# A decoder block in split-float products: two more units with Strassen steps, a new opening order, and a reordered last normalisation

## The chip, the cores and the metric

The kernel runs on one core of one Trainium2 chip. The metric is the device time of one execution in microseconds; three runs of the kernel before gave 2355.65 to 2356.98 with a median of 2356.65. Engines are named as in the profile: PE is the tensor engine (PEld its weight loads), DVE the vector engine, ACT the scalar engine, POOL the GpSimd engine, SP the engine that issues most DMAs.

## The reference, cut to what matters

```python
h = rmsnorm(x, norm_w)                                   # x: 256 tokens x 4096
proj = einsum('bsd,de->bse', h, w_in)                    # 4096 -> 20480
u_p, z_p, u_c, b_c, c_c, z_c, g_logit = split(proj)      # six of 2048, one of 8192
y_pool = causal_multiscale_pool(u_p, pool_w, pool_scale) * silu(z_p)
v = c_c * u_c                                            # causal convolution of width 3
y_conv = b_c * (conv_b + sum(conv_w[k] * shifted(v, k))) * silu(z_c)
br = einsum('bsnc,ncd->bsnd', stack(y_pool, y_conv), w_branch)
merged = sum(sigmoid(g_logit + gate_b) * br, over the two branches)
x = x + einsum('bsd,de->bse', merged, w_out)
return rmsnorm(x, final_norm_w)
```

All arrays are float32. `rmsnorm(x, w)` is `x * rsqrt(mean(x*x) + 1e-6) * w` over the 4096 channels of a token.

## The kernel before

**Products.** Each float32 operand is split into a high and a low part of the PE's rounded float format, and a product is three matmuls: high x high, high x low, low x high. ACT writes the high parts (`highs`), DVE subtracts to get the low parts (`lows`). A matmul is 128x128 weights against 128x512.

**Units and steps.** The work is a list of units, each 1024 output columns for all 256 tokens: cz0, cb0, cu0, cc0, then cz1 to cc1 (convolution branch: z, b, u and c columns), pz0, pu0, pz1, pu1 (pooling branch), eight gate units g, eight branch units b0_0, b1_0, b0_1 and so on, and four output units o0 to o3. A unit of the input or output product has 16 steps, a branch unit has 8; a step takes 256 rows of the weight matrix. The unit's string of letters says which steps are plain pairs (`P`: 8 block products, 24 matmuls) and which are one Strassen-Winograd step (`S`: 7 block products, 21 matmuls). An S step costs DVE and ACT more: besides the highs and lows of the weight tile (three ring cells) it needs four sums of its quarters in the tile `parts`, and their highs and lows (four more cells). The activations' side of an S step needs its own sums (`x_sums` in the opening, `Fill` later).

**The bank scheme.** Plain products accumulate in four banks (`sums`), S steps in these and in four more (`shared`). When a unit's products for a bank are complete, ACT copies the bank out (`evacuate` for the first four, into E or Y; `copy_corners` for the others, into J), DVE adds up J (`corner_sums`), and `combine` adds J to the unit's result: on DVE, or for units marked `late` by two accumulating DMAs on POOL (`gather`). Units marked `late` apply the input norm's factor `rin` afterwards; the first unit, which has no S step, applies it in `evacuate`.

**Order.** Every engine runs its instructions in the order written; the program is one long list made at build time. After each group of three matmuls `after_group` writes what has become due: bank copies, corner sums, then one entry of the `queue` of the previous unit's closing work (an entry, a tick, per six matmuls), one step of a `Fill`, and then `pump`, which issues weight loads (three raw tiles of 1 MiB) and the preparation of coming steps, up to four ahead, as far as the ring's 15 cells reach: four for a P, three and then four for an S. A P step gives back a cell after its second, fourth, sixth and eighth group, an S step one after each group. In a unit's last step `pump` is left out for some groups so that bank copies are not queued behind preparation:

```python
after_group(u, g[0], st, st is u.steps[-1] and st.kind == "P" and 3 <= i < len(gs) - 1)
```

Units with an `urgent` function prepare only `lead` steps ahead during their last step.

**The opening.** The first unit also prepares the activations: `x_direct` for the eight pairs that stay plain (two ACT copies and two DVE instructions), `x_scale` on ACT and `x_sums` on DVE for the eight Strassen operands (number 8 to 15), each written one step ahead. `FIRST` is the order of the 16 operands. In steps 4, 7, 10 and 13 a quarter of x is fetched into E, in steps 6, 9, 12 and 15 squared and summed (one half on ACT, one on DVE), and behind step 15 `root` computes `rin`.

**The end.** The last unit's last three steps are done token half by token half (t = 0, 1), the second one also column half by column half. `finish_half` adds a bank to E, squares it on ACT with a sum into `ossq`, and multiplies by the final weights; `finish` turns the five partial sums into `rout` by reduce, scale, square root and one Newton step, scales four column quarters by it and writes them.

Of the kernel before, what the change touches and what calls it, by code (L numbers as in the profile page):

```python
# [15 lines left out]
P = 128  # L16
# [34 lines left out]
def hybrid_block(ctx: ExitStack, tc: tile.TileContext, x, xc, prm, rows_in, w_in, pool_w, w_branch, w_out, out):  # L51
# [488 lines left out]

    def silu_y(late):
        def silu(t):
            act(Y[:, t], Y[:, t], AF.Silu, **(dict(scale=rin[:, t:t + 1]) if late else {}))
        return gap(18 if late else 3) + [lambda: silu(0), None, lambda: silu(1)]

# [4 lines left out]
    def conv_units(c, first):  # L550
# [7 lines left out]
        def c_epi(u):  # L558
            def inner(j):
                if j == 3:  # L560
                    for i in range(4):
                        act(chan(E)[:, 2 * i:2 * i + 2], bankview(i))

            def outer(j):
                act(chan(J)[:, 2 * j:2 * j + 2], bankview(j))

            def taps(j):
                v, y = chan(E)[:, 2 * j:2 * j + 2], chan(Y)
                for i in range(2):
# [12 lines left out]
            return items + [None, lambda: mul(chan(E), chan(J), chan(Y)), lambda: put(y_d[1, c], chan(E))]  # L582

        u = in_unit(f"cz{c}", base + 3 * HALF, lambda u: silu_y(u.late) + (gap(4) + side_items(ND - 1) + side_items(ND - 2) if first else []),
                    FIRST if first else SIX5, dst=Y)
        u.late = not first
        in_unit(f"cb{c}", base + HALF, b_epi, TEN if c else NINE_A).late = True
        u = in_unit(f"cu{c}", base, lambda u: rescale(Y), NINE, dst=Y)
        u.late = True
        in_unit(f"cc{c}", base + 2 * HALF, c_epi, NINE_A).urgent = lambda: mul(E, E, Y)  # L590

    def pool_units(c):
        u = in_unit(f"pz{c}", HALF + c * NU, lambda u: silu_y(True) + gap(4) + band_items(c), HOST if c else SIX5, dst=Y)
        u.late = True
# [187 lines left out]
    class Fill:  # L782
        def __init__(self, o, src, free, ready):
            self.o, self.free, self.ready, self.src = o, free, ready, src
            self.at = self.st = None
            self.phase = self.due = 0
# [26 lines left out]
    def pop_fill(force=None):  # L813
        now[0] += 1
        for f in list(fills):
            if f.at is not None and f.free() and (now[0] >= f.at + LANDING or f.o is force):
                if f.advance(f.o is force):
                    break
# [53 lines left out]
    for _ in range(WARM):  # L872
        pin(nc.tensor.matmul(shared(3)[:, 0:2 * P], warm[:, 0:P], warm, start=True, stop=True))

    def rstd_of(q, r, name):
        a = q.shape[1]
        m = sb(f"{name}_m", [P, a])
        s = sb(f"{name}_s", [P, a])
        pin(nc.vector.tensor_reduce(out=m, in_=q, axis=mybir.AxisListType.X, op=ALU.add))
        pin(nc.vector.tensor_scalar(out=m, in0=m, scalar1=1.0 / D, scalar2=EPS, op0=ALU.mult, op1=ALU.add))  # L880
        act(s, m, AF.Sqrt)
        pin(nc.vector.reciprocal(out=r, in_=s))
        mul(m, m, r)
# [181 lines left out]
    def queue_fills():  # L1065
        for n in range(2):
            for i in [s.op for s in names[f"b{n}_0"].main]:
                j = y_ops[n].index(i)
                fills.append(Fill(i, y_d[n, j // 4][:, j % 4].rearrange("p k t -> p (k t)"), freed(i),
                                  lambda: True))  # L1070
# [27 lines left out]
    for u in units:  # L1098
# [28 lines left out]
        for st in u.steps:  # L1127
# [5 lines left out]
            if state["now"] == OPENED:  # L1133
                opening.close()
                sums = ctx.enter_context(tc.tile_pool(name="parts", bufs=1)).tile([P, 4, NH], F32, name="parts")
                open_side()
# [38 lines left out]
    def finish_half(t, n):  # L1175
        cs = slice(n * NH, (n + 1) * NH)
        add(E[:, t, cs], PE_[t][n], E[:, t, cs])
        act(sa[:, 4 * n:4 * n + 4].rearrange("p o c -> p (o c)"), E[:, t, cs], AF.Square,
            accum_out=ossq[:, t, 3 + n:4 + n])
        mul(rest[:, t, cs], E[:, t, cs], Y[:, 0, cs])  # L1180

    def finish(t):
        r = rout[:, t:t + 1]
        rstd_of(ossq[:, t:t + 1], r, f"rout{t}")
        for c in range(4):
            v = rest[:, t] if c == 3 else parked[c][:, t]
            if c == 1:
                act(v, v, scale=r)
            else:
                pin(nc.vector.tensor_scalar(out=v, in0=v, scalar1=r, scalar2=None, op0=ALU.mult))  # L1190
        for c in (1, 0, 2, 3):
            v = rest[:, t] if c == 3 else parked[c][:, t]
            queue_ = nc.scalar if c == 1 else nc.sync
            pin(queue_.dma_start(of[t * P:(t + 1) * P, c * NU:(c + 1) * NU], v))

# [51 lines left out]
```

## Time and profile before

| | |
|---|---|
| median of 3 runs | 2356.65 us |
| the profiled execution | 2356.82 us |
| its span, first to last instruction | 2354.7 us |
| mean granted PE clock | 0.999 |
| busy: PE, DVE, ACT, POOL | 2340.7, 2217.8, 1542.9, 139.0 us |
| matmuls | 10424 |
| DMA, mean over the span | 242 GB/s |

The profile is of one execution. A timeline row has the start, the time, the engine, the line, the operation with its tiles, the count of merged instructions, and in brackets the idle time of that engine in front of it with what ended it. A row of the chain of waits has start, time, engine and tile. A row of the windows view has the stretch, its length, then busy time and count for PE, PEld, DVE, ACT and POOL, the granted clock, and the DMA share and rate. Most helpers record under one line each: L58 is any ACT instruction, L61 any DVE tensor-tensor instruction, L73 scalar-tensor-tensor, L1026 the matmuls.

### The profile page before, as it was taken

The page shows a single profiled execution, that of the slowest core. Times are in us where ns is not written, and L with a number is a line of the kernel's source. Part 1 is how long each engine was busy: PE and PEld are TensorE (multiplying, and loading weights), DVE is VectorE, ACT ScalarE, POOL GpSimd, SP SyncE. Part 2 cuts the span into 40 slices and gives each one's busy share as a digit, 9 for nine tenths or more (in the row PEclk, how much of TensorE's full clock was granted, in tenths as well). Part 3 has the DMA queues.
Part 4 walks back from the last instruction along what each step waited for, and adds up shares of the span by engine and source line. Part 5 has one row for each costly group of instructions (what it writes and reads, how often), then busy time and mean ns, then how long its engine had stood idle before and what let it go on. Part 6 is the DMA issues. An engine that isn't in the chain of part 4 may idle for free.

```text
span 2354.7 us, 28337 instructions
## 1 busy us (share of the span) xinstructions
PE 2340.7 (99%) x10424; PEld 1938.7 (82%) x10424; DVE 2217.8 (94%) x2454; ACT 1542.9 (66%) x1841; POOL 139.0 (6%) x195
## 2 busy tenths in 40 slices
PE   9999999999999999999999999999999999999998
PEld 7888888888888888888888888888888888888886
DVE  8899989999979979979999999998999899999998
ACT  6666756766656666666677767677666566566664
POOL 0000000000001000100000000001101001000000
PEclk9999999999999999999999999999999999999999
DMA  9667655776656656656787787778767678767877
GB/s 351 231 234 248 217 201 215 251 232 233 222 207 216 219 196 213 220 198 222 242 258 254 256 265 246 250 267 283 258 225 247 254 247 282 250 206 263 260 255 279
DMA packets 95387, 569.44 MB, mean 242 GB/s; under 512 B 10320, under 2 KB 10576, under 8 KB 34832
## 3 DMA queue, kind: packets, MB, share of 16 engines
q1 hardware_dynamic: 69824, 485.39, 56.7%
q0 software_dynamic: 24848, 81.01, 13.7%
q8 instruction: 81, 1.33, 0.2%
q10 hardware_dynamic: 576, 1.24, 0.1%
q14 instruction: 58, 0.48, 0.1%
HBM read 521.46 MB, written 25.17 MB: 232 GB/s over the span
## 4 chain that ended last, share of the span: by engine, by line
PE 97%; DVE 1%; DMA 0%; ACT 0%; issue 0%; DVEq 0%; SPq 0%; ACTq 0%
PE sums L1026 70%; PE shared L1026 25%; PE shared L676 1%; PE shared L462 1%; DVE ring L61 1%; DMA raw<-in_w_branch_dram 0%; DVE parts L61 0%; DMA raw<-in_w_in_dram 0%; ACT ring L58 0%; DVE arena L61 0%; PE shared L652 0%; DVE J L61 0%; ACT E L58 0%; PE shared L653 0%; PE shared L655 0%
## 5 line engine op out<-in xcount | busy, mean ns | idle before, releaser
L1026 PE MATMUL sums<-ring,arena 128*128 128x512 f32 x7011 | 1640.7, 390 | 1.9 <-ACT E L58 1.1
L1026 PEld LDWEIGHTS sums<-ring,arena 128*128 128x128 f32 x7011 | 1315.3, 188 | 275.5 <-ACT E L58 1.5
L61 DVE TENSOR_TENSOR ring<-raw,ring 128x1024 fp32r<-128x1024 f32 (+2 forms) x887 | 962.2, 1104 | 70.4 <-ACT ring L58 69.5
L58 ACT ACTIVATE ring<-raw 128x1024 fp32r<-128x1024 f32 (+3 forms) x682 | 785.5, 1192 | 210.2 <-PE sums L1026 98.5
L58 ACT ACTIVATE ring<-parts 128x512 fp32r<-128x512 f32 (+1 forms) x683 | 510.4, 761 | 510.2 <-DVE parts L61 438.3
L1026 PE MATMUL shared<-ring,arena 128*128 128x512 f32 x2241 | 541.1, 389 | 0.0
L61 DVE TENSOR_TENSOR ring<-parts,ring 128x1024 fp32r<-128x1024 f32 (+1 forms) x475 | 524.5, 1146 | 8.7 <-ACT ring L58 8.7
L1026 PEld LDWEIGHTS shared<-ring,arena 128*128 128x128 f32 x2241 | 420.6, 188 | 87.3
L61 DVE TENSOR_TENSOR parts<-parts,raw 128x512 f32<-128x512 f32 x444 | 303.3, 683 | 0.0
L61 DVE TENSOR_TENSOR parts<-raw 128x1024 f32<-128x1024 f32 x222 | 270.2, 1217 | 10.9 <-DMA raw<-in_w_in_dram 6.0
L61 DVE TENSOR_TENSOR J<-J 128x512 f32<-128x512 f32 (+1 forms) x90 | 78.1, 868 | 6.0 <-ACT J L58 2.8
L1026 PE MATMUL sums<-ring,last_pair 128*128 128x512 f32 x306 | 76.2, 389 | 0.0
L58 ACT ACTIVATE J<-shared 128x512 f32<-128x512 f32 x128 | 69.5, 601 | 1.6
L1026 PEld LDWEIGHTS sums<-ring,last_pair 128*128 128x128 f32 x306 | 57.4, 188 | 11.9
L85 POOL DMA_DIRECT2D E<-J x28 | 34.2, 1463 | 479.5 <-ACT ring L58 300.1
L1026 PE MATMUL shared<-ring,last_pair 128*128 128x512 f32 x216 | 51.9, 389 | 0.0
L1026 PE MATMUL shared<-ring,side 128*128 128x512 f32 x207 | 50.7, 389 | 0.0
L1026 PEld LDWEIGHTS shared<-ring,last_pair 128*128 128x128 f32 x216 | 40.5, 188 | 8.4
L1026 PEld LDWEIGHTS shared<-ring,side 128*128 128x128 f32 x207 | 38.9, 188 | 8.1
L58 ACT ACTIVATE E<-sums 128x512 f32<-128x512 f32 x76 | 41.8, 592 | 4.5 <-PE sums L1026 2.7
L85 POOL DMA_DIRECT2D Y<-J x12 | 14.7, 1458 | 265.1 <-ACT ring L58 138.5
L58 ACT ACTIVATE E<-sums,rin 128x512 f32<-128x512 f32 x20 | 13.0, 689 | 13.9 <-PE sums L1026 13.9
(140 smaller groups left out, 645.6 us busy)
## 6 DMA issues: line engine op xcount, KB each, us to landing
raw<-in_w_in_dram SPq DMA_DIRECT2D x318, 1024.0 KB, 4.9
raw<-in_w_branch_dram SPq DMA_DIRECT2D x64, 1024.0 KB, 5.4
raw<-in_w_out_dram SPq DMA_DIRECT2D x64, 1024.0 KB, 4.8
E<-J POOLq DMA_DIRECT2D x28, 512.0 KB, 8.6
E<-in_rows_dram POOLq DMA_DIRECT2D x14, 512.0 KB, 9.8
Y<-J POOLq DMA_DIRECT2D x12, 512.0 KB, 9.3
gates_d<-E POOLq DMA_DIRECT2D x6, 1024.0 KB, 6.1
y_d<-E POOLq DMA_DIRECT2D x8, 512.0 KB, 5.2
```

What stands on the lines that cost most here:

```text
L58: return pin(nc.scalar.activation(dst, src, func, **kw))
L61: return pin(nc.vector.tensor_tensor(out=dst, in0=a, in1=b, op=op))
L85: return pin(nc.gpsimd.dma_start(dst, src, accum_op=ALU.add))
L462: pin(nc.tensor.transpose(shared(j)[:, i * T + t * P:i * T + (t + 1) * P], src[:, t, c:c + P], ident))
L676: pin(nc.tensor.matmul(o, a, b, start=(k, i) == (0, 0), stop=(k, i) == (3, 2)))
L1026: pin(nc.tensor.matmul(ps, lhs, rhs, start=n == 0, stop=n == u.total[b] - 1))
```

## The change

In the opening the order of the operands starts with four plain ones, the last two Strassen operands (14 and 15, steps 12 and 14) are now used in S steps, the squares are all on ACT, and steps 2 to 4 are split into halves. With S steps the first unit has corner banks, so it becomes `late`, its silu moves behind `gap(18)`, and the two side operands' work runs beside it; `parts` is allocated from the start. cb0 gets another order of its nine S steps, cz1 has seven S steps instead of six. The units cc0 and cc1 prepare three steps ahead in their last step, and the transposes of E behind them come two ticks later. In b0_0's closing step the first groups no longer call `pump`. Fills of the last quarter of `merged` may start after six ticks instead of twelve. At the end the sum of the first four partial sums is formed early, the square root is taken directly of scale times the fifth plus it, and two of the four column quarters are scaled and written in halves.

```diff
+SEVEN5 = "PPPPPSPSSPSPSSPS"
-FIRST = (0, 1, 8, 2, 9, 3, 10, 11, 4, 12, 13, 5, 14, 6, 15, 7)
+FIRST = (0, 1, 2, 3, 8, 4, 9, 5, 10, 11, 12, 13, 14, 6, 15, 7)
+FIRST_S = (14, 15)
+NINE_B = "PPPSSPSSPSSPSSPS"
...
+    sums = ctx.enter_context(tc.tile_pool(name="parts", bufs=1)).tile([P, 4, NH], F32, name="parts")
...
-            return [("P", i) for i in FIRST]
+            return [("S" if i in FIRST_S else "P", i) for i in FIRST]
...
-            items = [lambda: move(Y, g_d[c])] + gap(6) + pairs(transposes(E, inner)) + gap(5) + pairs(transposes(Y, outer))
+            items = [lambda: move(Y, g_d[c])] + gap(8) + pairs(transposes(E, inner)) + gap(3) + pairs(transposes(Y, outer))
...
+        def z_epi(u):
+            items = silu_y()
+            if first:
+                sides = gap(8) + side_items(ND - 1) + side_items(ND - 2)
+                items = [lambda a=a, b=b: (a and a(), b and b()) for a, b in zip(items + gap(len(sides) - len(items)), sides)]
+            return items
+
+        u = in_unit(f"cz{c}", base + 3 * HALF, z_epi, FIRST if first else SEVEN5, dst=Y)
+        u.late = True
+        in_unit(f"cb{c}", base + HALF, b_epi, TEN if c else NINE_B).late = True
...
-        in_unit(f"cc{c}", base + 2 * HALF, c_epi, NINE_A).urgent = lambda: mul(E, E, Y)
+        u = in_unit(f"cc{c}", base + 2 * HALF, c_epi, NINE_A)
+        u.urgent, u.lead = (lambda: mul(E, E, Y)), 3
...
+    for s in steps[2:5]:
+        s.halved = True
...
+    def mean_of(q, m):
+        pin(nc.vector.tensor_reduce(out=m, in_=q, axis=mybir.AxisListType.X, op=ALU.add))
+        pin(nc.vector.tensor_scalar(out=m, in0=m, scalar1=1.0 / D, scalar2=EPS, op0=ALU.mult, op1=ALU.add))
...
-        act(q[:, 0], q[:, 0], AF.Square, accum_out=ssq[:, 0, c:c + 1])
-        stt(q[:, 1], q[:, 1], 1.0, q[:, 1], ALU.mult, ALU.mult, accum_out=ssq[:, 1, c:c + 1])
+        for t in range(2):
+            act(q[:, t], q[:, t], AF.Square, accum_out=ssq[:, t, c:c + 1])
...
-                              lambda c=c: c in merged and now[0] >= merged[c]))
+                              lambda c=c: c in merged and now[0] >= merged[c], LANDING // (1 + c // 3)))
...
-            after_group(u, g[0], st, st is u.steps[-1] and st.kind == "P" and 3 <= i < len(gs) - 1)
+            after_group(u, g[0], st, st is u.steps[-1] and st.kind == "P" and (0 if u is names["b0_0"] else 3) <= i < len(gs) - 1)
...
             accum_out=ossq[:, t, 3 + n:4 + n])
+        if n == 0:
+            mean_of(ossq[:, t:t + 1, 0:4], known[:, t:t + 1])
         mul(rest[:, t, cs], E[:, t, cs], Y[:, 0, cs])
...
     def finish(t):
-        r = rout[:, t:t + 1]
-        rstd_of(ossq[:, t:t + 1], r, f"rout{t}")
-        for c in range(4):
-            v = rest[:, t] if c == 3 else parked[c][:, t]
+        r, last_, k = rout[:, t:t + 1], ossq[:, t, 4:5], known[:, t:t + 1]
+        act(dev[:, t:t + 1], last_, AF.Sqrt, scale=1.0 / D, bias=k)
+        stt(mean[:, t:t + 1], last_, 1.0 / D, k, ALU.mult, ALU.add)
+        refined(mean[:, t:t + 1], dev[:, t:t + 1], r)
+        pieces = []
+        for c, a, n in ((0, 0, NH), (1, 0, NH), (0, NH, NH), (1, NH, NH), (2, 0, NU), (3, 0, NU)):
+            v = (rest[:, t] if c == 3 else parked[c][:, t])[:, a:a + n]
             if c == 1:
                 act(v, v, scale=r)
             else:
                 pin(nc.vector.tensor_scalar(out=v, in0=v, scalar1=r, scalar2=None, op0=ALU.mult))
+            pieces.append((c, a, n, v))
```

`refined` holds the reciprocal and the Newton step that `rstd_of` had; the writes at the end then go piece by piece on the same queues as before (column quarter 1 on ACT's, the others on SP's).

More of the change, by code (lines that the diff above doesn't have):

```diff
@@ L539, in side_items, with silu_y @@
             lambda: move(side_d[i - ND + 2], side["tile"])]
-    def silu_y(late):
+    def silu_y():
         def silu(t):
-            act(Y[:, t], Y[:, t], AF.Silu, **(dict(scale=rin[:, t:t + 1]) if late else {}))
-        return gap(18 if late else 3) + [lambda: silu(0), None, lambda: silu(1)]
+            act(Y[:, t], Y[:, t], AF.Silu, scale=rin[:, t:t + 1])
+        return gap(18) + [lambda: silu(0), None, lambda: silu(1)]
     def rescale(d):
@@ L782, in hybrid_block, with __init__ @@
     class Fill:
-        def __init__(self, o, src, free, ready):
-            self.o, self.free, self.ready, self.src = o, free, ready, src
+        def __init__(self, o, src, free, ready, landing):
+            self.o, self.free, self.ready, self.src, self.landing = o, free, ready, src, landing
             self.at = self.st = None
@@ L815, in pop_fill @@
         for f in list(fills):
-            if f.at is not None and f.free() and (now[0] >= f.at + LANDING or f.o is force):
+            if f.at is not None and f.free() and (now[0] >= f.at + f.landing or f.o is force):
                 if f.advance(f.o is force):
@@ L878, in rstd_of, with refined @@
         s = sb(f"{name}_s", [P, a])
-        pin(nc.vector.tensor_reduce(out=m, in_=q, axis=mybir.AxisListType.X, op=ALU.add))
-        pin(nc.vector.tensor_scalar(out=m, in0=m, scalar1=1.0 / D, scalar2=EPS, op0=ALU.mult, op1=ALU.add))
+        mean_of(q, m)
         act(s, m, AF.Sqrt)
+        refined(m, s, r)
+    def refined(m, s, r):
         pin(nc.vector.reciprocal(out=r, in_=s))
@@ L1134, in hybrid_block @@
                 opening.close()
-                sums = ctx.enter_context(tc.tile_pool(name="parts", bufs=1)).tile([P, 4, NH], F32, name="parts")
                 open_side()
@@ L1190, in finish @@
                 pin(nc.vector.tensor_scalar(out=v, in0=v, scalar1=r, scalar2=None, op0=ALU.mult))
-        for c in (1, 0, 2, 3):
-            v = rest[:, t] if c == 3 else parked[c][:, t]
+            pieces.append((c, a, n, v))
+        for c, a, n, v in pieces:
             queue_ = nc.scalar if c == 1 else nc.sync
-            pin(queue_.dma_start(of[t * P:(t + 1) * P, c * NU:(c + 1) * NU], v))
+            pin(queue_.dma_start(of[t * P:(t + 1) * P, c * NU + a:c * NU + a + n], v))
     for t in range(2):
```

9 lines of the change are left out of this document (3 added, 6 removed).

## The prediction

> **What bounds the kernel now.** I read the busy line of the page first, then the chain of waits, then the places where the tensor engine (PE) is not dense.
>
> ```profile
> span 2354.7 us, 28337 instructions
> ...
> PE 2340.7 (99%) x10424; PEld 1938.7 (82%) x10424; DVE 2217.8 (94%) x2454; ACT 1542.9 (66%) x1841; POOL 139.0 (6%) x195
> ```
>
> The chain ended last runs through PE almost throughout; two of its pieces:
>
> ```profile
> 102.08 2.72 PE shared L1026 x12
> 104.81 7.48 PE sums L1026 x33
> ```
>
> Both give 0.2267 us a matmul (2.72/12, 7.48/33). A plain pair (P) has 24, so 5.44 us; a Strassen step (S) has 21, so 4.76 us. 10,424 at 0.2267 would be 2363, and the span is below that only because transposes and band products are shorter: there is hardly a gap to take. The timeline of PE shows the exceptions:
>
> ```profile
> 5.98 16.55 PE L1026 MATMUL sums<-ring,arena 128*128 128x512 f32 x63 [0.83 <-DVE ring L774]
> 22.36 0.84 PE L1026 MATMUL sums<-ring,extra 128*128 128x512 f32 x3
> ...
> 1718.30 12.58 PE L1026 MATMUL sums<-ring,arena 128*128 128x512 f32 x54 [1.07 <-ACT E L58]
> ```
>
> From 5.98 to 22.36 there are 63 matmuls in 16.38 us; at full pace they take 14.28, so 2.1 us go to a slow start. At 1718.30, between b0_0 and b1_0, PE waits 1.07 us for ACT to copy a bank out. The third loss is the end: PE's last result releases DVE at 2343.76 (row further down), and 11 us of the span remain. Everything the change can win lies in the number of matmuls, these two places and the end; what it can lose lies with DVE (94% busy) and the order on ACT.
>
> **Matmuls.** Steps 12 and 14 of cz0 and one step of cz1 turn from P into S: 3 x 3 matmuls x 0.2267 = **-2.04 us**. That holds only if DVE and ACT prepare the steps in time.
>
> **The first unit's DVE work.** Costs from its timeline, start to start, since neighbours overlap by 0.08:
>
> ```profile
> 30.10 1.01 DVE L61 TENSOR_TENSOR sa<-sa 128x128 f32<-128x128 f32 x4
> ...
> 33.29 1.22 DVE L73 SCALAR_TENSOR_TENSOR E<-E 128x1024 f32<-128x1024 f32 x1
> ...
> 34.43 2.29 DVE L61 TENSOR_TENSOR ring<-raw,ring 128x2048 fp32r<-128x2048 f32 x1
> 36.63 0.61 DVE L61 TENSOR_TENSOR sa<-sa 128x128 f32<-128x128 f32 x2
> ...
> 66.33 0.87 DVE L73 SCALAR_TENSOR_TENSOR arena<-Y,par,arena 128x256 fp32r<-128x256 f32 x2
> 67.12 2.28 DVE L61 TENSOR_TENSOR ring<-raw,ring 128x2048 fp32r<-128x2048 f32 x1
> ...
> 84.57 1.22 DVE L61 TENSOR_TENSOR parts<-raw 128x1024 f32<-128x1024 f32 x1
> ...
> 88.92 1.22 DVE L61 TENSOR_TENSOR ring<-parts,ring 128x1024 fp32r<-128x1024 f32 x1
> 90.55 1.23 DVE L61 TENSOR_TENSOR ring<-parts,ring 128x1024 fp32r<-128x1024 f32 x1 [0.41 <-ACT ring L58]
> ```
>
> A set of x sums takes 33.29 - 30.10 = 3.2, the square 1.1, the low parts of a pair 2.2 (34.43 to 36.63), the low part of a plain x 0.8 (66.33 to 67.12), a Strassen step 88.92 - 84.57 = 4.35 and two lows of 1.1 and 1.2, together 6.6, of which I count 0.3 as waiting for ACT (the last row has such a wait, 0.41) that a fully queued DVE would not have: 6.3 us.
>
> The lows of step 6 end at 36.7 in both kernels: before, DVE's square stood in front of them; after, both squares are on ACT in front of step 6's highs (rows below), and DVE waits for these instead. From there to the lows of step 15 DVE now has: three plain x (2.4), seven pairs' lows (15.4), six x sums (19.2), two Strassen steps (12.6): 49.6 us, so 86.3, with the lows of step 15 the last 2.2. These must wait for ACT: its last copy of step 14 ends some 1.6 us before DVE ends that step (behind DVE's last add stand two lows of 1.2 on DVE and one copy of 0.6 on ACT), near 81.8, and then it has the x scale, two squares and the first half of the highs ahead.
>
> ```profile
> 31.14 1.07 ACT L58 ACTIVATE E<-E 128x1024 f32<-128x1024 f32 x1 [3.49 <-DMA E<-in_x_dram]
> ...
> 32.20 1.90 ACT L58 ACTIVATE ring<-raw 128x2048 fp32r<-128x2048 f32 x1
> 34.00 0.89 ACT L58 ACTIVATE sa<-Y,par 128x256 f32<-128x256 f32 x2
> ...
> 79.47 0.20 ACT L58 ACTIVATE rin_s<-rin_m 128x2 f32<-128x2 f32 x1 [1.33 <-DVE rin_m L880]
> ...
> 93.28 2.73 ACT L58 ACTIVATE Y<-sums,rin 128x512 f32<-128x512 f32 x4 [2.77 <-PE sums L1026]
> 95.91 2.00 ACT L58 ACTIVATE ring<-raw 128x1024 fp32r<-128x1024 f32 x2
> ```
>
> 0.9 + 2 x 1.1 + 1.0 (half of 1.9) brings ACT to 85.9, and the lows of step 15 end near **88**. PE starts step 15 (row 89.68 below, less 1.36 for six matmuls) at 88.3; the pair is taken in halves, so no stall yet. But before, the sqrt that follows these lows ran at 79.47, ten us ahead of PE's 89.68; now DVE is level with PE.
>
> **Who is late next: the copies out of the banks between cz0 and cb0.** Before, ACT sat idle 2.77 us for the end of cz0 and copied the next unit's third pair only afterwards (the last two rows above). After, cb0 begins PPPS. The ring has 15 cells and the last step and two pairs hold 12; the third pair needs four, and the fourth comes free after the second of the last step's eight groups. Its highs are thus issued there, ahead of the bank copies (issued from the fifth group on); `hold` spares only groups four to seven. Cz0 now has Strassen banks too, so four copies into J stand in the same queue. ACT's order after the lows of step 15 is: the sqrt, highs of cb0's first pair, two J, second pair, two J, third pair, bank copies. Queue prices:
>
> ```profile
> 1713.40 1.07 ACT L58 ACTIVATE J<-shared 128x512 f32<-128x512 f32 x2
> 1715.76 1.49 ACT L58 ACTIVATE ring<-raw 128x1536 fp32r<-128x1536 f32 x1 [1.29 <-DMA raw<-in_w_branch_dram]
> 1717.15 0.61 ACT L58 ACTIVATE arena<-sb 128x512 fp32r<-128x512 f32 x1
> 1717.67 2.04 ACT L58 ACTIVATE E<-sums 128x512 f32<-128x512 f32 x4
> ```
>
> ```profile
> 89.68 12.40 PE L1026 MATMUL sums<-ring,arena 128*128 128x512 f32 x54
> ```
>
> 88.0 + 0.6 (sum, scale, sqrt) + 3 x 1.9 + 4 x 0.53 = 96.4, and the first bank is out 0.6 later, at 97.0. PE ends cz0 at 89.68 - 1.36 + 24 x 0.2267 = 93.8 and needs that bank at once. Stall **+3.2 us**. Bounds: 1.4 if the wait at step 6 falls away (by the same prices DVE is there 1.8 us earlier than ACT's highs); 4.6 if each Strassen step costs the plain sum of its rows (6.9); 0 if ACT gets the highs done before DVE reaches level, for which nothing in the rows speaks. The four bank copies are 0.5 apart and PE's groups 0.68, so only the first counts. What remains in the first unit costs nothing: the squares on ACT outside step 15, the halves of steps 2 to 4 (0.1 us each) and the J sums on DVE, which in cb0's three pairs needs 2.2 of 5.44 us; the silu 18 ticks (108 matmuls, 24 us) later behind two gathers on POOL, since its reader is a unit away; the earlier `parts` tile, which has no instruction; the side fills, whose first use is cb1.
>
> **Seven Strassen steps in cz1.** DVE gets 6.3 - 2.2 = 4.1 us more and PE 0.68 less.
>
> ```profile
> 337.88:368.72 30.84, 30.84 (x153) 25.84 (x152) 24.23 (x22) 18.52 (x24) 0.58 (x1) 1.00 0.56 206
> 368.72:424.48 55.76, 55.76 (x247) 46.17 (x246) 55.08 (x68) 35.74 (x46) 1.51 (x2) 1.00 0.62 226
> 424.48:504.88 80.40, 80.40 (x356) 66.60 (x355) 80.17 (x89) 54.89 (x66) 3.06 (x3) 1.00 0.68 229
> ```
>
> DVE (third busy figure) idles 6.6 us in the five pairs that open cz1, 0.7 in its rest, 0.2 in cb1. The extra work falls in the rest, and cb1 gives nothing back: 4.8 - 0.7 = 4.1 us must come out of the run-ahead. Bounds 0 and 4.1; I take **+0.5**, near the low end, since the idle opening shows that the ring and not DVE set the run-ahead there. The lead of three puts one pair's lows (2.2 us) ahead of the product that the transposes read; they are moved two ticks (12 matmuls, 2.7 us), so they still find it: 0.
>
> **The closing step of b0_0.** The wait at 1718.30 comes from the highs at 1715.76, three cells of a Strassen step, held by their weight DMA, ahead of the bank copies. They need 3 free cells and have them when the step *before* the closing one ends; in the closing step nothing fits until its last group. So the new `hold` stops nothing: **0**, between -1.3 (the gap and the 0.1 after it) and +0.5 (a fill copy like that at 1717.15 changing sides). Last fills sooner: the unit o0 shows no PE gap, **0**.
>
> **The end.**
>
> ```profile
> 2341.14 0.74 DVE L1190 TENSOR_SCALAR parts<-parts,rout 128x1024 f32<-128x1024 f32 x1
> 2341.80 0.68 DVE L61 TENSOR_TENSOR E<-sums,E 128x512 f32<-128x512 f32 x1
> 2342.51 0.69 DVE L61 TENSOR_TENSOR parts<-E,Y 128x512 f32<-128x512 f32 x1
> 2343.76 0.69 DVE L61 TENSOR_TENSOR E<-sums,E 128x512 f32<-128x512 f32 x1 [0.55 <-PE sums L1026]
> ```
>
> ```profile
> 2344.48 0.73 ACT sa L58 x2
> ...
> 2345.24 0.17 DVE rout_m L879
> ...
> 2345.62 0.21 ACT rout_s L58
> ```
>
> ```profile
> 2347.41 0.99 SPq L1194 DMA_DIRECT2D out_dram<-raw  x2
> ```
>
> The chain loses reduce and scalar, 2345.24 to 2345.62: -0.38. But `mean_of` is put between the first half's add and its product, and waits for ACT's square: 0.73 + 0.38 = 1.1 us in DVE's queue, with the product, the second half's add and through it the second square behind it. For the first 128 rows that gives 1.1 - 0.38 = +0.75, plus 0.1 for a fourth scaling instruction; the add at 2341.80 follows the scaling at once, so it moves to 2342.65. Its product comes 0.7 (add) + 1.1 later, at 2344.5, and the second half's add 0.65 behind that (as 2341.80 stands to 2341.14), at 2345.1 instead of 2343.76: +1.35. Less 0.38, r is 0.95 late. The first piece is half as wide (0.37 instead of 0.74), so the first output DMA leaves at 2348.0 instead of 2347.41. After it 2 MiB flow out, which sets the end in both kernels. **+0.7** with an estimated 0.1 for packets of half the size; bounds -0.7 (both gains, the wait hidden) and +1.0.
>
> **Sum.** -2.04 + 3.2 + 0.5 + 0 + 0.7 = +2.4. The profiled execution took 2356.82 (span 2354.7 and 2.1 around it), 0.17 above the median, so it would be 2359.2 and the median **2359.0 us**.
>
> **Rivals.** *A, ACT is in time* at cz0's end: for it that ACT is busy for only 66% of the span; against it that it idles before DVE's results, which come late. -2.04 + 0.5 + 0.7 = 2355.8. *B, slower by more than the bound*: the gap at 93.8 lets PE's clock fall. The trace has 1.07 us without that (54 matmuls from 1718.30 at full pace) and the slow start at 5.98; the slow stretch cost 2.1 us. With the stall at its upper bound: -2.04 + 4.6 + 2.1 + 0.5 + 0.7 = +5.9, 2362.5. It decides from a gap somewhere above 1.07 us. [...] *C, the closing step does what its name says*, with no stall at cz0 and the end's wait hidden: -2.04 - 1.3 - 0.4 = 2352.9; against it the count of ring cells.
>
> **How the numbers follow.** Forecast 0.5, A 0.24, B 0.2, C 0.06. The range leaves out C and the worst of B: 2354.6 to 2362.6; the forecast's own is 2357.0 to 2360.5. The bound is 0.2%, about what a measurement tells here: 4.7 us, 2351.9 and 2361.4. Faster only by part of C, 0.03; slower by B and a little of the forecast's edge, 0.21; within, 0.76.
>
> **What would show it.** 10,415 matmuls. A gap of 2 to 4 us on PE near 94 us, released by ACT's copy into Y, with a copy of 2048 wide just before it; a faster pace without gap shows A; a row of slow matmuls behind it shows B. The wait before b1_0's first matmul still there. On DVE in the last 20 us, a wait for ACT before each `mean_of`, and the first SP issue of the last rows later after PE's last matmul than 3.7 us. Wrong overall if PE stays dense at 94 us, or if it stalls within cb1.

## The result and the profile after

The changed kernel takes 2368.76 us (median of 5 runs, 2365.21 to 2369.61) against 2356.65 (5 runs, 2355.65 to 2358.03) for the kernel before: a ratio of 1.0047, 95% interval 1.0036 to 1.0058. It is slower by 12 us; 2359.0 was forecast, in a range up to 2362.6. The profiled execution took 2369.61. Its page begins:

```profile
span 2367.9 us, 28401 instructions
...
PE 2345.7 (99%) x10415; PEld 1938.7 (82%) x10415; DVE 2229.2 (94%) x2480; ACT 1554.0 (66%) x1874; POOL 141.4 (6%) x197
```

The 9 matmuls fewer are there, and yet PE is busy 5 us longer: besides waiting, PE must have run slower somewhere. Following the start of each unit's first matmul through both timelines of PE shows where the 13.2 us of span came in:

| first matmul of | before | after | difference | what was added since the line above |
|---|---|---|---|---|
| cb0 | 95.12 | 97.68 | +2.56 | 6 matmuls fewer (-1.36), an opening at full clock (-1.4), two gaps in cz0 (+5.0), a slower pace and small waits (+0.3) |
| cu0 | 176.04 | 181.65 | +5.61 | slow matmuls (+2.9), the slower pace |
| cb1 | 424.48 | 429.94 | +5.46 | 3 matmuls fewer in cz1 (-0.68), a slower pace (+0.5) |
| b0_0 | 1674.91 | 1682.85 | +7.94 | the slower pace (+2.5) |
| b1_0 | 1718.30 | 1727.20 | +8.90 | a longer gap |
| b0_1 | 1759.95 | 1770.46 | +10.51 | slow matmuls |
| o0 | 2014.29 | 2025.62 | +11.33 | a gap of 0.66 at its start |
| (last matmul) | 2343.33 | 2355.10 | +11.77 | the slower pace |
| (end of span) | 2354.7 | 2367.9 | +13.2 | the end |

**The gaps in cz0.** PE's timeline, and below it ACT's, of the changed kernel:

```profile
87.06 0.40 PE L1045 MATMUL sums<-ring,arena 128*128 128x512 f32 x1
88.11 5.51 PE L1045 MATMUL sums<-ring,arena 128*128 128x512 f32 x23 [0.65 <-DVE ring L64]
97.68 7.57 PE L1045 MATMUL sums<-ring,arena 128*128 128x512 f32 x20 [4.06 <-ACT Y L61]
```

```profile
89.50 0.20 ACT L61 ACTIVATE rin_s<-rin_m 128x2 f32<-128x2 f32 x1 [0.46 <-DVE rin_m L890]
89.61 1.90 ACT L61 ACTIVATE ring<-raw 128x2048 fp32r<-128x2048 f32 x1
91.42 1.06 ACT L61 ACTIVATE J<-shared 128x512 f32<-128x512 f32 x2
92.37 2.00 ACT L61 ACTIVATE ring<-raw 128x512 fp32r<-128x512 f32 x2
94.27 1.08 ACT L61 ACTIVATE J<-shared 128x512 f32<-128x512 f32 x2
95.22 1.92 ACT L61 ACTIVATE ring<-raw 128x2048 fp32r<-128x2048 f32 x1
97.02 2.07 ACT L61 ACTIVATE Y<-sums 128x512 f32<-128x512 f32 x4
```

This is the queue that the prediction wrote down, instruction by instruction. PE has issued its last matmul of cz0 and waits 4.06 us for the first copy into Y; ahead of that copy stand three preparations of cb0 and four copies into J.

**The slow matmuls.** 20 matmuls in 7.57 us, in the row at 97.68, are not 0.2267 us each. Single starts show 12 distances of 427 ns among them, behind a first one of 591. The windows view has the granted clock as the third figure from the right:

```profile
93.00:97.00 4.00, 0.62 (x3) 0.19 (x1) 3.96 (x5) 4.00 (x4) 0.00 (x0) 0.96 0.57 201
97.00:104.00 7.00, 6.32 (x16) 5.03 (x17) 6.97 (x7) 4.20 (x7) 3.09 (x3) 0.53 0.95 274
104.00:120.00 16.00, 16.00 (x72) 13.24 (x71) 11.08 (x13) 7.55 (x10) 0.00 (x0) 1.00 0.78 250
...
1727.00:1733.00 6.00, 5.80 (x18) 4.62 (x19) 5.96 (x11) 4.03 (x8) 0.54 (x1) 0.72 0.53 147
```

The granted clock is halved for 6.83 us behind this gap (96.71 to 103.54), and once more, for 3.41 us, behind the one at the end of b0_0. There ACT's queue is the one of before (a copy of highs that waits for its weight transfer, a fill's copy, then the banks), only later against PE:

```profile
1721.54 1.06 ACT L61 ACTIVATE J<-shared 128x512 f32<-128x512 f32 x2
1724.66 1.49 ACT L61 ACTIVATE ring<-raw 128x1536 fp32r<-128x1536 f32 x1 [2.06 <-DMA raw<-in_w_branch_dram]
1726.05 0.61 ACT L61 ACTIVATE arena<-sb 128x512 fp32r<-128x512 f32 x1
1726.57 2.04 ACT L61 ACTIVATE E<-sums 128x512 f32<-128x512 f32 x4
```

```profile
1727.20 6.00 PE L1045 MATMUL sums<-ring,arena 128*128 128x512 f32 x18 [2.03 <-ACT E L61]
```

Before, PE waited 1.07 us here and kept its clock; now 2.03, and eight matmuls follow at 427 ns. Read side by side, the two traces put the delay down to DVE, which hardly idles from 1688 us on (busy for 38.14 of the 39 us to 1727): one fill's low part (0.68 us), written ahead of a pair's lows before, now stands behind them, and everything after it on DVE is 0.7 us later, the raw tile's release and the weight transfer with it. No run moves that fill alone.

**The slower pace.** The view of one tile's matmuls (minimum, median and maximum duration), of the kernel before and of the changed one:

```profile
L1026 PE MATMUL sums<-ring,last_pair x306: 388/389/398, 84.2 to 2343.3; 128*128 128x512 f32 x153
L1026 PE MATMUL shared<-ring,last_pair x216: 389/389/390, 162.4 to 2250.2; 128*128 128x512 f32 x108
```

```profile
L1045 PE MATMUL sums<-ring,last_pair x291: 392/395/397, 82.2 to 2355.1; 128*128 128x512 f32 x146
L1045 PE MATMUL shared<-ring,last_pair x228: 395/396/397, 83.6 to 2261.7; 128*128 128x512 f32 x114
```

Every matmul with weights in `last_pair` lasts 6 to 7 ns longer, and their starts lie 233 ns apart instead of 226.7; over the 544 distances between starts that they take part in, this is 3.5 us. The other tiles keep their pace: the median with weights in `arena` and in `side` is 389 ns in both kernels. `last_pair` is one of the tiles that the diff does not name. But the new end has `rout_k`, `rout_m` and `rout_s` where the old one had four such tiles, each takes 32 bytes per partition, and `last_pair` lies below them: it moved from byte 187392 to 187424.

**The end.** DVE's rows behind the last matmul, whose start is at 2355.10:

```profile
2355.80 0.16 DVE L889 TENSOR_REDUCE rout_k<-ossq 128x1 f32<-128x4 f32 x1 [0.79 <-ACT sa L61]
2355.99 0.15 DVE L890 TENSOR_SCALAR rout_k<-rout_k 128x1 f32<-128x1 f32 x1
2356.06 0.68 DVE L64 TENSOR_TENSOR parts<-E,Y 128x512 f32<-128x512 f32 x1
2356.66 0.68 DVE L64 TENSOR_TENSOR E<-sums,E 128x512 f32<-128x512 f32 x1
```

The reduce waits 0.79 us for ACT's square, and the product and the add of the last half stand behind it: the add starts 1.56 us after the last matmul's start, before it was 0.43.

### The profile page after: what moved, and what is told of

It reads as the page before. It is cut to its first block, busy times and chain, and to the rows that moved or that the text cites. A ratio compares the mean times of both kernels' runs of the same rounds, so it can differ in the third digit from the quotient of the medians.

```text
span 2367.9 us, 28401 instructions
## 1 busy us (share of the span) xinstructions
PE 2345.7 (99%) x10415; PEld 1938.7 (82%) x10415; DVE 2229.2 (94%) x2480; ACT 1554.0 (66%) x1874; POOL 141.4 (6%) x197
## 4 chain that ended last, share of the span: by engine, by line
PE 94%; DVE 3%; ACT 1%; DMA 1%; issue 0%; SPq 0%; DVEq 0%; ACTq 0%
PE sums L1045 67%; PE shared L1045 25%; DVE ring L64 1%; PE shared L687 1%; PE shared L466 1%; ACT ring L61 1%; DMA raw<-in_w_in_dram 1%; DVE parts L64 0%; DMA raw<-in_w_out_dram 0%; DMA raw<-in_w_branch_dram 0%; DVE arena L64 0%; ACT E L61 0%; ACT J L61 0%; DVE J L64 0%; ACT sa L61 0%
## 5 line engine op out<-in xcount | busy, mean ns | idle before, releaser
L64 DVE TENSOR_TENSOR ring<-raw,ring 128x1024 fp32r<-128x1024 f32 (+3 forms) x900 | 962.3, 1088 | 79.9 <-ACT ring L61 79.2
L61 ACT ACTIVATE ring<-parts 128x512 fp32r<-128x512 f32 (+1 forms) x694 | 517.6, 759 | 533.4 <-DVE parts L64 468.2
L1045 PE MATMUL shared<-ring,arena 128*128 128x512 f32 x2265 | 546.8, 389 | 0.0
L64 DVE TENSOR_TENSOR ring<-parts,ring 128x1024 fp32r<-128x1024 f32 (+1 forms) x480 | 531.6, 1149 | 8.6 <-ACT ring L61 8.6
L1045 PEld LDWEIGHTS shared<-ring,last_pair 128*128 128x128 f32 x228 | 42.8, 188 | 10.4
L61 ACT ACTIVATE E<-E 128x1024 f32<-128x1024 f32 x20 | 20.9, 1045 | 3.5 <-DMA E<-in_x_dram 3.5
```

The source lines that it names most:

```text
L61: return pin(nc.scalar.activation(dst, src, func, **kw))
L64: return pin(nc.vector.tensor_tensor(out=dst, in0=a, in1=b, op=op))
L1045: pin(nc.tensor.matmul(ps, lhs, rhs, start=n == 0, stop=n == u.total[b] - 1))
```

## The experiments

### The place of last_pair

Theory P: the pace depends on where the weights lie. Rival: it depends on what else uses the memory at the time. Two kernels move nothing but the place, in opposite directions:

```diff
 # a1_pad: the changed kernel
     known, mean, dev = (sb(f"rout_{k}", [P, 2]) for k in "kms")
+    sb("pad", [P, 8])
 # a2_shift: the kernel before, rout0_m and rout1_m in one tile
-        m = sb(f"{name}_m", [P, a])
+        m = sb(f"{name}_m", [P, a]) if name == "rin" else one.setdefault("m", None)
+        if m is None:
+            m = one["m"] = sb("rout_m", [P, 2])
+        if name != "rin":
+            m = m[:, int(name[-1]):int(name[-1]) + 1]
```

> The changed kernel with one unused 32-byte tile more in the pool that holds rout_k, so that last_pair lies at byte 187392 of its partition again, as before, instead of 187424; nothing else differs. Theory P (the place of the weights sets their matmuls' pace): the 544 matmuls with weights in last_pair go back from 233 ns to 226.7 ns, 544 x 6.3 ns = 3.4 us less, about 2365.3 us against the changed kernel's 2368.8. Rival (those matmuls are slow because of what DVE, ACT or transfers do beside them): they stay at 233 ns and the time at 2368.8.

> The kernel before with one 32-byte tile less (rout0_m and rout1_m share one tile), so that last_pair lies at 187424; nothing else differs. Theory P: its last_pair matmuls go from 226.7 to 233 ns and the time rises by 3.4 us to about 2360.1. Rival: 226.7 ns and 2356.7 as before.

Measured: a1_pad 2361.17 us (ratio to before 1.0018, 1.0009 to 1.0027), a2_shift 2361.07 (1.0019, 1.0010 to 1.0028). The pace follows the place both ways; of a1_pad and of a2_shift:

```profile
L1045 PE MATMUL sums<-ring,last_pair x291: 388/389/389, 83.3 to 2346.9; 128*128 128x512 f32 x146
```

```profile
L1032 PE MATMUL sums<-ring,last_pair x306: 392/395/397, 85.2 to 2347.8; 128*128 128x512 f32 x153
```

So P holds. But the unused 32 bytes bring 7.6 us, twice the 3.5 that the pace explains. The two profiles, 8.4 us apart, show the rest in waits: with the pad PE idles 1.57 us at the end of b0_0 and the clock stays (-0.5 and -1.5), seven matmuls are at 427 ns behind the gap at 93 instead of 13 (-1.2), that gap ends 0.5 sooner, and the gap at the start of o0 is gone (-0.7). How much of this is the place and how much is chance, the next two parts bear on. a2_shift, too, lost more than the pace: 4.4 us, with a new PE wait of 0.70 us near 1763.

What "place" means was left to a stream of such matmuls by themselves, with both operands moved:

```diff
+    for w, m in PLACES:                      # in elements of 4 bytes
+        for i in range(64):
+            matmul(bank, weights[:, w:w + 128], fixed[:, m:m + 512], ...)
```

> No part of the reference's work: dense stretches of 64 matmuls of the kernel's shape with the weights or the moving operand moved by 0 to 1024 bytes, each place twice in opposite order. The first such run showed 226.7 ns with both at multiples of 512 bytes or both 32 bytes off, but 232 to 234 with the weights alone 32, 64, 96 or 128 bytes off. Theory D (what counts is the distance of the two places): equal moves of both stay at 226.7, unequal ones go to 229 to 234, and a move of the weights alone by 512 or 1024 bytes is as good as none. Rival (each operand's own place): equal moves are as slow as single ones. Rival (order in the run, not place): the two passes differ.

Three of its timeline's rows: both operands at multiples of 512 bytes; the weights 32 bytes off; both 32 bytes off.

```profile
42.61 14.22 PE L47 MATMUL bank<-fixed,weights 128*128 128x512 f32 x62
...
57.13 14.62 PE L47 MATMUL bank<-fixed,weights 128*128 128x512 f32 x62
...
262.95 14.24 PE L47 MATMUL bank<-fixed,weights 128*128 128x512 f32 x62
```

Less the last one's 0.39 us, over 61 steps: 226.7, 233.3 and 227.0 ns. Theory D holds in all 22 places and both passes: with the weights 32, 64, 128, 192, 256, 384 and 512 bytes further than the moving operand's offset the pace is 233.3, 233.3, 232.4, 228.9, 226.7, 232.3 and 226.7 ns, and with equal moves it is 226.7 to 227.2. In these places the pace goes with the distance of the two operands modulo 256 bytes. In the kernel the arena (from byte 2560), the ring (from 88576) and the side tile (from 179200) are multiples of 512, so only `last_pair` was off. The distance costs up to 6.6 ns a matmul in this run (233.3 against 226.7); by what mechanism, no run shows.

### The first unit

Theory Q: the highs queued ahead of the bank copies make the gap, and the gap makes the clock fall. p_first is the kernel before with the first unit's part of the diff alone; f_nos is the changed kernel with `FIRST_S = ()`; f_hold lets the hold reach further, in the changed kernel with the pad:

```diff
+    def held(u, st, i, n):
+        if st is u.steps[-1] and st.kind == "P":
+            return (0 if u.name in ("cz0", "b0_0") else 3) <= i < n - 1
+        return st is u.steps[-2] and (u.name == "cz0" or u.name == "b0_0" and i == n - 1)
...
-            after_group(u, g[0], st, st is u.steps[-1] and ...)
+            after_group(u, g[0], st, held(u, st, i, len(gs)))
...
-            pump()
+            if not (u.name in ("cz0", "b0_0") and st is u.steps[-2]):
+                pump()
```

> The kernel before with the first unit's part of the change alone (new order, two S steps, cb0 as PPPSSPSSPSSPSSPS, the scale of the silu, the first steps halved, both squares on ACT). Theory Q (bank copies behind preparation on ACT, then a halved clock): 6 matmuls less (-1.4), a gap of 4 to 5 us near 93 us and 0.9 near 87 (+5.1), 13 or 14 matmuls at 427 ns behind it (+3.0): about 2363.4. Rival, the forecast's own sizes (gap 3.2, clock kept): 2358.5. Rival, the slow matmuls in the changed kernel's profile were chance and not tied to the gap: 2360.4.

> The changed kernel with its new order of the first unit but no S step in it; everything else as in the changed kernel. Theory Q: with P steps alone DVE and ACT keep ahead of PE, no gap near 93 us, no slow matmuls behind it, 6 matmuls more (+1.4): 2368.8 - 4.2 - 0.9 - 3.0 + 1.4 = about 2362. Rival (the highs of the next unit ahead of the bank copies make the gap, whatever the step kinds): a gap of 2 us or more stays at the end of the unit and the time is 2366 or more.

> The changed kernel with the pad of 32 bytes, and with a hold that holds: no preparation is issued from the start of cz0's step 14 (an S) to its last bank, and none between b0_0's last S step and its last bank. Against the kernel with the pad alone (2361.2 us). Theory Q (the highs queued ahead of the bank copies on ACT make both gaps): cb0's first matmul 3 us sooner (94 instead of 97.2 us), no slow matmuls behind it, the gap at the end of b0_0 1.5 us shorter (2.0 to about 0.5), a stall of at most 0.5 us at cb0's second or third step: about 2356. Rival (the held preparation is then late and the stall only moves into cb0 or b1_0): new gaps of 2 us or more inside these units, 2360 or more.

Measured: p_first 2360.54 us (11 runs from 2358.26 to 2361.95; ratio to before 1.0015, 1.0006 to 1.0024), f_nos 2361.11, f_hold 2356.61 (ratio to before 0.9997, 0.9988 to 1.0006; 4.6 below a1_pad). PE's rows at that place in p_first, in f_nos and in f_hold, and ACT's in f_hold:

```profile
97.25 12.99 PE L1037 MATMUL sums<-ring,arena 128*128 128x512 f32 x56 [3.08 <-ACT Y L60]
```

```profile
88.72 21.47 PE L1045 MATMUL sums<-ring,arena 128*128 128x512 f32 x94
```

```profile
87.93 5.51 PE L1045 MATMUL sums<-ring,arena 128*128 128x512 f32 x23 [0.60 <-DVE ring L64]
93.81 6.41 PE L1045 MATMUL sums<-ring,arena 128*128 128x512 f32 x27 [0.37 <-ACT Y L61]
```

```profile
89.43 1.90 ACT L61 ACTIVATE ring<-raw 128x2048 fp32r<-128x2048 f32 x1
91.24 2.04 ACT L61 ACTIVATE J<-shared 128x512 f32<-128x512 f32 x4
93.14 2.09 ACT L61 ACTIVATE Y<-sums 128x512 f32<-128x512 f32 x4
95.05 5.25 ACT L61 ACTIVATE ring<-raw 128x512 fp32r<-128x512 f32 x4
```

Without S steps there is no gap at all. With them, and two of the three preparations moved behind the bank copies, the 3.47 us of a1_pad (4.06 in the changed kernel) become 0.37 and the clock stays. The gap's cause is shown. The rival for f_hold, that the held preparation is late then, is right in kind but not in size: a new gap of 0.53 us stands inside b1_0, and PE idles 1.0 us between b1_0 and b0_1. The hold in b0_0 that holds removed that unit's gap entirely. The diff's own hold cannot do so: with its 0 in place of 3 every engine's instructions stay the same, in the same order.

p_first came out 2.9 us below Theory Q, at the 2360.4 of the rival that calls the slow matmuls chance: in its profile the gap is 3.08 us, and not one matmul behind it is slow. So a gap does not always make the clock fall. But that profile is of an execution of 2358.69 us, 1.85 below the median; no trace shows whether the clock fell in the slower ones. The spread points the same way: the middle half of p_first's times spans 2.3 us and of a1_pad's 2.2, of f_hold's 0.9.

### The clock

micro makes pauses of known length in a stream of the kernel's matmuls, four times each:

```diff
+    for width in WIDTHS:                     # 64 to 4096 columns, four rounds
+        bank = dense(64 + 3 * (k % 5), late)             # 64 to 76 matmuls
+        activation(tag[:, k % 8:k % 8 + 1], bank[:, 0:1], AF.Copy)
+        activation(late[:, 0:width], lines[:, 1, 0:width], AF.Copy)
```

> No part of the reference's work: matmuls of the kernel's shape (128x128 weights, 128x512 moving, both fp32r) in dense stretches of 64 and more, first with the weights or the moving operand moved by 0 to 128 bytes, then with pauses made by an ACT copy of 64 to 4096 columns on which the next stretch waits, four times each length (from the profile's rows of ACT, 0.6 us for 512, 1.04 for 1024, 1.9 for 2048 columns, about 0.6 to 4.6 us idle). Theory P: weights 32 bytes off an address that is a multiple of 64 take 233 ns, at multiples of 64 226.7. Rival: the same at all places. Clock, theory R (some idle time between 1.07 us, which left the clock alone in the kernel before, and 2.03 us, which halved it in the changed kernel): matmuls at 427 ns follow every pause of 2 us and more, none of 1 us and less. [...] Rival (a share of fixed windows of 3.4 us): pauses of the same length between 1 and 3 us do it in some of the four cases and not in others.

Its first part, on places, missed: with the weights 64 and 128 bytes off a matmul took 233.3 and 232.4 ns, not 226.7, and with both operands 32 bytes off some 227. That led to micro2. For the pauses, five of its PE rows follow; at full pace 64, 67 and 70 matmuls take some 14.7, 15.4 and 16.0 us:

```profile
408.15 15.48 PE L47 MATMUL bank<-late,weights 128*128 128x512 f32 x67 [1.84 <-ACT late L58]
425.58 16.16 PE L47 MATMUL bank<-late,weights 128*128 128x512 f32 x70 [1.95 <-ACT late L58]
443.81 16.40 PE L47 MATMUL bank<-late,weights 128*128 128x512 f32 x64 [2.06 <-ACT late L58]
...
758.69 16.41 PE L47 MATMUL bank<-late,weights 128*128 128x512 f32 x64 [2.06 <-ACT late L58]
777.58 15.48 PE L47 MATMUL bank<-late,weights 128*128 128x512 f32 x67 [2.48 <-ACT late L58]
```

Slow matmuls follow none of the 44 pauses up to 1.84 us, 2 of 4 at 1.95, 3 of 4 at 2.06, at 2.48 and at 2.91, all at 3.34 and 3.76. They come 6 to 9 at a time, once 14. Theory R (every pause of 2 us) does not fit; the rival of a share of fixed windows does: pauses of one length, from 1.95 to 2.91 us, were followed by slow matmuls in some of the four cases and not in others. The following counts show what differs: how much of one fixed stretch is idle.

How much, the traces tell. In every trace the changes of clock lie on one grid of 3.413 us, to within 5 ns, so each trace can be cut into the fixed stretches. Behind the first rise of the clock and up to the last matmul, all 24 full-clock stretches in which PE idled 1.95 us or more were followed by one at half clock; none of those with 1.81 us or less was; of two with 1.88 us, one was. Stretches of p_first at its gap, of the changed kernel at its gap, and of micro at a pause of 3.77 us:

```profile
92.48:95.90 3.42, 1.70 (x8) 1.08 (x6) 3.42 (x4) 3.42 (x5) 0.00 (x0) 1.00 0.58 153
95.90:99.31 3.41, 2.06 (x9) 1.71 (x10) 3.34 (x4) 3.41 (x6) 0.41 (x1) 1.00 1.01 428
```

```profile
93.30:96.71 3.41, 0.32 (x2) 0.00 (x0) 3.41 (x4) 3.41 (x4) 0.00 (x0) 1.00 0.50 163
96.71:100.12 3.41, 2.44 (x6) 1.98 (x7) 3.34 (x4) 3.41 (x6) 0.79 (x2) 0.50 1.00 416
```

```profile
833.79:837.21 3.42, 1.54 (x7) 0.94 (x5) 1.85 (x2) 0.00 (x0) 1.00 0.00 0
837.21:840.62 3.41, 1.53 (x7) 1.27 (x8) 1.83 (x1) 0.00 (x0) 1.00 0.02 5
840.62:844.04 3.42, 3.42 (x10) 2.68 (x9) 0.00 (x0) 0.00 (x0) 0.50 0.00 0
```

The gap of p_first is split into 1.72 and 1.35 us of idle, and neither half is enough; the changed kernel's puts 3.09 us into one stretch, and with 0.97 us still idle in the next one the clock stays low for a second (three half-clock stretches with 0.79 us or more of idle were followed by another, none with 0.57 or less). So a pause under 1.88 us did nothing in these traces. One above 3.76, twice 1.88, would put that much into one stretch wherever it falls (an estimate from these counts; in micro all eight pauses of 3.34 and 3.76 were followed by slow matmuls), and between them it goes by where it falls. A stretch of 3.413 us holds eight matmuls of 427 ns, in keeping with the 6 to 9 behind a pause.

### Seven Strassen steps, and the fills

p_seven is the kernel before with `SEVEN5` in cz1 alone; f_land is a1_pad with the old delay, `LANDING`, for all fills:

```diff
 # f_land
-  lambda c=c: c in merged and now[0] >= merged[c], LANDING // (1 + c // 3)))
+  lambda c=c: c in merged and now[0] >= merged[c], LANDING))
```

> The changed kernel with the pad, and the last fills as late as before (LANDING for all). Theory L (the sooner fills have no part in the time): 2361.2 as with the pad alone, no gap at the start of o0 either way. Rival (they move transfers and copies into the way of the last unit before o0): a difference of 1 us, seen in the gap at the start of o0.

> The kernel before with seven S steps in cz1 and nothing else. Theory V (the seventh S itself costs nothing, but the 3 matmuls less shift the planner's due times, so that the last fill of o0 comes late, as in the two kernels with the old LANDING that have it): 3 matmuls less (-0.7) and a gap of about 1.4 us inside o0 released by DVE's write of the arena (+1.2): 2357.2. Rival (the gap in o0 came from the hold or the end, not from the seventh S): 2356.0 and no gap in o0.

Measured: f_land 2363.41 us (2.2 above a1_pad), p_seven 2359.79 (ratio to before 1.0011, 1.0002 to 1.0020). Theory L falls and V holds in kind; PE's row inside o0 in p_seven, and in f_land:

```profile
2096.97 1.89 PE L1027 MATMUL sums<-ring,arena 128*128 128x512 f32 x7 [1.06 <-DVE arena L62]
```

```profile
2101.68 1.89 PE L1045 MATMUL sums<-ring,arena 128*128 128x512 f32 x7 [1.00 <-DVE arena L64]
```

With cz1's seventh S and the old fills the last operand of o0 comes late; neither the kernel before nor p_first, which lack that S, has this gap. The sooner fills take it away. The profiles of f_land and a1_pad lie 3.2 us apart: 1.3 are this gap, and the rest is the gap at 93 us, which ends 0.7 later and has 13 slow matmuls behind it instead of 7. p_seven ends 2.6 us above V's 2357.2; in its profile, against that of before, b0_1 begins 0.7 us later by a gap ahead of it, cz1 is 0.5 longer than its fewer matmuls make it, cb0 begins 0.4 later, and the span ends 12.0 us after the last matmul's start instead of 11.3. What lengthens this end was not found.

### The end, and two versions

f_mean is a1_pad with `mean_of` behind the product; best_a is the kernel before with `SEVEN5`, the hold that holds in b0_0, the pad and this end; best_b is f_hold with this end and the hold from the first group in b1_0 too.

```diff
-        if n == 0:
-            mean_of(ossq[:, t:t + 1, 0:4], known[:, t:t + 1])
         mul(rest[:, t, cs], E[:, t, cs], Y[:, 0, cs])
+        if n == 0:
+            mean_of(ossq[:, t:t + 1, 0:4], known[:, t:t + 1])
```

> The changed kernel with the pad, and with mean_of behind the product of the first half instead of ahead of it. Theory E (at the end, the add of the last half waits on DVE behind mean_of, which waits for ACT's square): that add starts 0.4 us after the last matmul's start instead of 1.6 and everything behind it comes 1.1 us sooner: 2360.1 against 2361.2 with the pad alone. Rival (the last output transfers set the end): no change.

> The kernel before with seven S steps in cz1, the hold that holds in b0_0 alone, the changed end with mean_of behind the product, and the pad (last_pair at 187392); the first unit stays as before. Theory: 3 matmuls less (-0.7), the gap of 1.5 us at the end of b0_0 nearly gone (-1.2), the shorter root chain (-0.3): about 2354.4 against 2356.65. Rival (cz1's seventh S makes cb1 stall by up to 4 us, or the held preparation of b1_0 is late): 2357 to 2361.

> The changed kernel with the pad, the hold that holds in cz0 and b0_0, the same hold in b1_0's closing step (its bank copies stood behind a copy of b0_1's highs that waited for its transfer), and mean_of behind the product. Against the kernel with the hold alone (2356.6 us): the gap of 1.4 us between b1_0 and b0_1 nearly gone (-1.0), the end 1.1 sooner: about 2354.5, 0.1% faster than the kernel before (2356.8). Rival (the next late preparation takes the gap's place): 2355.5 to 2356.5.

Measured: f_mean 2360.56 us (0.6 below a1_pad), best_a 2358.52 (ratio to before 1.0007, 0.9998 to 1.0016), best_b 2355.50 (0.9992, 0.9983 to 1.0000). f_mean's DVE row, with the last matmul's start at 2347.38:

```profile
2347.83 0.68 DVE L64 TENSOR_TENSOR E<-sums,E 128x512 f32<-128x512 f32 x1
```

0.45 us behind it, as Theory E has it, and the span ends 11.5 us after that start instead of 12.6 in f_hold, which has the old order. The median shows only half of this; the gap at 93 us, where the clock's part goes by chance, may hide the rest (not shown). best_a missed its forecast: it kept the old `LANDING`, and so has the gap in o0 that p_seven has; its hold in b0_0 worked and the wait came back as 1.6 us between b1_0 and b0_1. best_b came out as its rival has it: PE is dense from b1_0 into b0_1 and waits 1.39 us at 1775 instead. It lies 1.5 us under the kernel before, at the edge of what can be told from no change.

## Why the prediction was wrong, step by step

The profiled execution lies 10.4 us above the 2359.2 forecast for it. The terms below add up to about that: the clock 4.5, the place of a tile 3.5, b0_0's wait 1.0, cz0's stall 0.7, the end 0.7, a gap at the start of o0 0.8, less the 0.5 that cz1 did not need.

- **Matmuls, -2.04**: right; 10,415.
- **The stall at the end of cz0, +3.2**: the mechanism was right down to the order on ACT, the size near. cb0 began 2.56 us late where -1.36 + 3.2 = 1.84 was forecast: DVE's lows of step 15 ended at 89.2 and not at 88, and PE waited for their first half too (0.65 us, to 88.11). The gaps themselves are longer than the stall forecast, since PE reached them 1.4 us sooner by the opening; that moved the wait and not the time.
- **The clock**: the step that failed. The forecast took the stall without it, and B, with it, had 0.2. Its price of 2.1 us was near (2.9 here, some 1.6 for eight slow matmuls elsewhere), its place right. The condition was wrong: that a stall of 3.2 us leaves the clock alone and one of 4.6 does not was the author's estimate, and no run showed it. In these traces the clock fell when some 1.9 us of a pause lay in one stretch of 3.413; the changed kernel's gap put 3.09 us into one. A stall of 3.2 us that falls anywhere on the grid escapes only in (3.76 - 3.2)/3.413, about one case in six (an estimate from micro's and the kernels' stretches). So, by that estimate, a stall of the forecast's size has, more often than not, a price like the 1.6 and 2.9 us measured.
- **b0_0's closing step, 0**: the hold indeed stops nothing. But the bounds asked only what the hold does, and not what the shifted order of all later work does: 0.96 us of gap, and 1.6 of clock behind it.
- **The place of a tile, no term at all**: 3.5 us, and the largest single term after the clock. The line with `rout_k`, `rout_m` and `rout_s` was read as free.
- **cz1's seventh S, +0.5, and the fills, 0**: together 0, as the changed kernel's dense cb1 and the inside of its o0 show. Singly they are not: the S makes o0 wait 1.4 us, which the sooner fills remove.
- **The end, +0.7**: the wait was right, the size 1.4: the add of the last half came 1.13 us later (1.35 forecast), the shorter root chain gave back 0.3 (0.38 forecast), and the last landing stands 0.5 us further from the end of the span, which no step had. The forecast's 0.1 for smaller packets is seen in no run by itself.
- **The opening's slow start, "2.1 us go"**: it costs nothing. p_seven has the full clock there and waits 1.8 us for DVE at 19.4 instead; cz0 ends at 95.65, in the kernel before at 95.28. The changed kernel, too, has the full clock there (20 matmuls from 8 to 12 us, 15 in the kernel before) and is 1.4 us ahead, which the gap at the end of cz0 takes back.

What stays open: why the distance of two operands matters to PE, and what makes the 0.66 us gap at the start of o0, which the pad takes away. Part of the changed kernel's 2365.2 to 2369.6 may be where its gaps fall on the clock's grid. The mean clock of each run, 0.996 in the three from 2368.76 up and 0.997 in the two below, fits this; it is too coarse to show it.

## What to carry to other kernels

When a diff changes how many small tiles are allocated, ask which big tile moves, and compare the median duration of one kind of matmul by tile before and after. Price a gap on PE with what the clock did behind gaps of its size: here about 1.6 us for each stretch of 3.413 us at half clock (eight matmuls at 427 instead of 226.7 ns), behind 11 of the 16 pauses from 1.95 to 2.91 us and all eight of 3.34 and 3.76 in micro. To keep bank copies prompt, look at what stands in front of them on their engine when the unit's last step begins; a hold in the last step is too late for what was written in the step before.

## What the hardware showed that was not expected

In micro and micro2, weights and moving operand at a distance that is no multiple of 256 bytes cost 228.9 to 234.3 ns a matmul instead of 226.7 in all places tried but one (weights 16 bytes further on, 226.7). In micro the clock fell for 6 to 9 matmuls of 427 ns (once 14) behind 19 of the 24 pauses of 1.95 to 3.76 us and behind none up to 1.84: in these traces what counted was some 1.9 us of idle PE within one stretch of a fixed grid of 3.413 us. And 32 unused bytes made the changed kernel 7.6 us faster, with the kernel before at 2356.65 beside both.
